# Two-layer decoder trunk on one core: the feed-forward's slab jobs handed out five at most at a time, partial sums parked through SyncE's queue, finished columns turned between slab jobs

## The chip, the core and the metric

The kernel runs on one core of one Trainium2 chip, in one launch. The metric is device time in microseconds (us), the median of three runs. A profile of one execution is read beside it. TensorE is called PE here (PEld is its weight load), VectorE DVE, ScalarE ACT, GpSimd POOL and SyncE SP, as in the profile.

## What is computed

The input has 256 tokens of width 2048. Each of two layers adds an attention-like mixer and then a feed-forward to the residual stream. The change concerns the feed-forward alone:

```
def squared_relu_mlp(h, w1, w2):
    z = jax.nn.relu(h @ w1)
    return (z * z) @ w2
...
        x = x + jnp.concatenate([token_out, mem_out], axis=-1) @ w_out[i]
        x = x + squared_relu_mlp(rms_norm(x, ffn_norm[i]), w_ff1[i], w_ff2[i])
```

`h` is 256x2048, `w1` 2048x8192 and `w2` 8192x2048, all float32. The kernel splits every float32 operand into a high part rounded to the fast matmul type and a low remainder, and adds the products high*high, low*high and high*low.

## The kernel before

All weights come from one DRAM array `in_w`, laid out in the order of use. The class `Feed` loads them through SP's queue into SBUF, ACT casts each block to its high part (line 170) and DVE subtracts to get the low part (line 173). The parts go into a ring of six 512-column places (`hi_ring`, `lo_ring`) and, in the feed-forward, two more (`slot`). Preparation runs at most three entries ahead of use.

The feed-forward (`ffn`) of a layer works on these pieces:

- **Up tiles** `("f", j)`, 64 of them. Each makes 128 of the 8192 hidden features with 32 matmuls into the PSUM bank `x_bank` (lines 919 and 921). ACT copies the bank out, and some 10 instructions on DVE and ACT, spread over the next ticks, turn two tiles into the squared values `z` (`convert`). A tick is four weight blocks of a tile, so an up tile has four.
- **Slab jobs** `("s", p, i, j)`. The product with `w2` is not done column by column: for most of it a Strassen-like scheme needs seven products in place of eight. One slab is the 2x2 block step for hidden chunk pair `i`: four jobs of 6, 3, 6 and 6 matmuls into seven PSUM banks `p` (lines 1010 to 1012). Its weights are a sum of blocks, so a slab needs two 512 KB loads through SP, `ra` and `rb`, and one 256 KB load that POOL's queue adds onto `ra` (line 141). Three SBUF buffers serve all slabs, so the `ra` of a slab can only be loaded when the slab two before it has been prepared to its last job.
- **Phases.** The seven banks hold one half of the output columns (A or B) for a run of slabs: `PHASES` lists half, first and last `i`. At the end of a phase `finish_banks` combines the seven banks on DVE and ACT into four corners (`c_x`, `c_y` and two parts of `room`; `c_a` and `c_b` in the last phase). If the half goes on later, the corners are parked in DRAM (`part`). If it has been parked before, the old sums are added back by accumulating loads on POOL's queue (called the gather here). When a half is complete, ACT scales the corners (line 1067), PE transposes them into the bank `ct`, and DVE adds them to the residual (line 1079); these steps are the turns.
- **Down tiles** `("d", 3, n)`, eight ordinary tiles at the end that use the hidden chunks that phase B leaves out.

`ffn_plan` writes the order: a credit of `RATE` = 4 jobs a tile is spent in the gap ahead of each up tile, a slab may start four tiles after its hidden pair was made, and the credit kept is at most 8. Steps that are written for a later time (`at(d, fn)`) run `d` ticks on. A scheduler below then orders each engine's instructions by its own estimates, so the place of an instruction in the queue of its engine is not simply that of the text.

An "end" below is the time around the end of a phase. Each layer has five: in this kernel after slab 7 (A), 14 (B), 21 (A), 24 (B, complete) and 32 (A, complete). Since all seven banks have to be emptied, a new phase starts one up tile later. Ahead of phase five the plan waits for four tiles (`hold = t + 4`), in which the B half is turned through the bank `t`.

While the feed-forward runs, half of the residual (`resid.parts[1]`, 1 MB) is stored to DRAM as `kept` (line 836), its SBUF place serves as two more spots for `z`, and it is loaded back at line 1112.

## Time and profile before

| | |
|---|---|
| median of three runs | 2095.45 us (2085.93 to 2096.34) |
| the profiled execution | 2087.09 us, its span 2085.2 us |
| PE busy | 2031.4 us, 97% |
| DVE, ACT, POOL busy | 85%, 66%, 9% |
| DMA | 439.80 MB, mean 211 GB/s |
| mean granted clock of TensorE | 0.991 |

The span is read in stretches: a row of the view by stretches gives its length, the busy time of each engine with the number of instructions in brackets, the mean granted clock (1.00 is full), the share of the DMA engines' time in use, and GB/s. The chain view follows the end of the program back from wait to wait; each row is a start in us, a length in us and what ran. A row such as "DMA slab<-in_w" is a transfer from its issue to its landing. Layer 0's feed-forward lies at about 236 to 963 us, layer 1's at about 1345 to 2085 us.

### The profile page before, as it was taken

How to read it: one execution, taken by the hardware profiler on the slowest of the kernel's cores; microseconds unless marked ns; L12 is line 12 of the kernel's file. 1: busy time of each engine (PE TensorE's matmuls, PEld its weight loads, DVE VectorE, ACT ScalarE, POOL GpSimd, SP SyncE). 2: the span in 40 equal slices, each digit the busy share in tenths (PEclk: the TensorE clock that was granted, in tenths of full speed). 3: DMA queues.
4: the chain of work that ended last, by engine and by line, in shares of the span. 5: the costliest groups of instructions: out<-in, count | busy, mean ns of one | idle time of the engine just before them, and what ended most of it. 6: DMA issues, size and time to landing. Idle time of an engine off the chain costs nothing.

```text
span 2085.2 us, 30357 instructions
## 1 busy us (share of the span) xinstructions
PE 2031.4 (97%) x10592; PEld 1713.7 (82%) x10592; DVE 1771.7 (85%) x2641; ACT 1373.1 (66%) x2177; POOL 178.8 (9%) x215
## 2 busy tenths in 40 slices
PE   9999999999999899999999999999999999999998
PEld 8888888788788687887888899888878878778787
DVE  8988788899889798998775798878889989888897
ACT  7765566576566566668665697566666666666664
POOL 0002300000000100000000000410000000101000
PEclk9999999999999999999999999999999999999999
DMA  8565666678677777676656645566677777868575
GB/s 310 176 205 186 217 213 209 208 228 233 209 224 230 212 225 209 213 206 202 213 184 195 194 144 177 192 223 212 209 220 234 223 217 225 233 211 241 177 224 171
DMA packets 133738, 439.80 MB, mean 211 GB/s; under 512 B 15248, under 2 KB 18320, under 8 KB 133072
## 3 DMA queue, kind: packets, MB, share of 16 engines
q1 hardware_dynamic: 112896, 395.90, 57.1%
q0 software_dynamic: 20544, 41.95, 11.0%
q8 instruction: 83, 1.36, 0.3%
q14 instruction: 71, 0.58, 0.1%
q10 hardware_dynamic: 144, 0.01, 0.0%
HBM read 424.56 MB, written 10.49 MB: 209 GB/s over the span
## 4 chain that ended last, share of the span: by engine, by line
PE 86%; DMA 5%; DVE 5%; ACT 2%; issue 2%; POOL 0%; DVEq 0%; ACTq 0%; POOLq 0%; SPq 0%
PE x_bank L919 19%; PE x_bank L921 9%; PE p L1012 7%; PE p L1010 7%; PE p L1011 7%; PE wo L503 6%; DMA slab<-in_w 3%; PE ff L919 3%; PE wo L505 3%; PE k L534 3%; PE v L534 3%; PE q L534 3%; PE u L503 2%; PE mk L534 2%; PE mv L534 2%
## 5 line engine op out<-in xcount | busy, mean ns | idle before, releaser
L173 DVE TENSOR_TENSOR lo_ring<-raw,hi_ring 128x512 fp32r<-128x512 f32 (+1 forms) x643 | 555.0, 879 | 108.2 <-ACT hi_ring L170 99.8
L170 ACT CAST hi_ring<-raw 128x512 fp32r<-128x512 f32 (+1 forms) x643 | 482.8, 766 | 202.8 <-PE wo L503 62.7
L170 ACT CAST hi_ring<-slab 128x1024 fp32r<-128x1024 f32 (+1 forms) x336 | 304.4, 906 | 135.6 <-DVE slab L204 60.9
L173 DVE TENSOR_TENSOR lo_ring<-slab,hi_ring 128x1024 fp32r<-128x1024 f32 (+1 forms) x336 | 346.9, 1043 | 44.2 <-ACT hi_ring L170 42.0
L141 POOL DMA_DIRECT2D slab<-in_w x112 | 97.2, 868 | 1655.5 <-DMA slab<-in_w 700.6
L170 ACT CAST slot<-slab 128x1024 fp32r<-128x1024 f32 x112 | 117.4, 1049 | 159.4 <-PE x_bank L919 109.4
L173 DVE TENSOR_TENSOR slot<-slab,slot 128x1024 fp32r<-128x1024 f32 x112 | 137.0, 1223 | 86.2 <-ACT slot L170 86.0
L919 PE MATMUL x_bank<-fx,hi_ring 128*128 128x512 f32 x664 | 209.4, 396 | 0.0
L503 PE MATMUL wo<-cat,hi_ring 128*128 128x512 f32 x512 | 161.6, 396 | 0.0
L921 PEld LDWEIGHTS x_bank<-fx,lo_ring 128*128 128x128 f32 x664 | 124.8, 188 | 29.5
L919 PE MATMUL x_bank<-fx0b,hi_ring 128*128 128x512 f32 x448 | 140.9, 395 | 0.0
L204 DVE TENSOR_TENSOR slab<-slab,slab 128x1024 f32<-128x1024 f32 x112 | 136.5, 1219 | 0.2
L933 ACT COPY room<-x_bank 128x512 f32<-128x512 f32 x112 | 65.4, 584 | 108.1 <-PE x_bank L921 108.1
L921 PE MATMUL x_bank<-fx,lo_ring 128*128 128x256 f32 x664 | 131.6, 278 | 0.0
L505 PEld LDWEIGHTS wo<-cat,lo_ring 128*128 128x128 f32 x512 | 96.1, 188 | 22.0
L919 PEld LDWEIGHTS x_bank<-fx,hi_ring 128*128 128x128 f32 x664 | 102.7, 189 | 4.9 <-ACT room L933 3.0
L173 DVE TENSOR_TENSOR slot<-raw,slot 128x1024 fp32r<-128x1024 f32 x70 | 85.5, 1222 | 19.7 <-ACT slot L170 19.5
L505 PE MATMUL wo<-cat,lo_ring 128*128 128x256 f32 x512 | 101.7, 278 | 0.0
L921 PEld LDWEIGHTS x_bank<-fx0b,lo_ring 128*128 128x128 f32 x448 | 84.2, 188 | 19.9
L1010 PE MATMUL p<-hi_ring,zb 128*128 128x512 f32 x230 | 91.0, 396 | 1.1 <-ACT hi_ring L170 0.9
L1011 PE MATMUL p<-hi_ring,zb 128*128 128x512 f32 x230 | 89.9, 391 | 0.0
L1012 PE MATMUL p<-lo_ring,zb 128*128 128x512 f32 x230 | 89.0, 390 | 0.0
(537 smaller groups left out, 4832.4 us busy)
## 6 DMA issues: line engine op xcount, KB each, us to landing
raw<-in_w SPq DMA_DIRECT2D x500, 512.0 KB, 4.4
slab<-in_w SPq DMA_DIRECT2D x224, 512.0 KB, 3.5
slab<-in_w POOLq DMA_DIRECT2D x112, 256.0 KB, 4.8
part<-room POOLq DMA_DIRECT2D x6, 512.0 KB, 3.8
resid_b<-kept SPq DMA_DIRECT2D x2, 1024.0 KB, 6.6
room<-part POOLq DMA_DIRECT2D x4, 512.0 KB, 8.4
memraw<-in_mem SPq DMA_DIRECT2D x4, 512.0 KB, 3.7
memraw<-in_mem SPq DMA_DIRECT2D x6, 256.0 KB, 6.0
```

Of the source, the lines that this page charges most:

```text
L141: self.nc.gpsimd.dma_start(t[:, 512:1024], self.wst[other, :, 512:1024], accum_op=ALU.add)
L170: cast = self.nc.scalar.copy(hi, src)
L173: self.nc.vector.tensor_sub(lo, src, hi.bitcast(F32))
L204: add(two, t.unsqueeze(1).to_broadcast([P, 2, 512]), two)
L503: nc.tensor.matmul(ps, hi, xs[:, k, :], start=first and j == 0, stop=False)
L505: nc.tensor.matmul(ps[:, T : 2 * T], lo, xs[:, k, 0:T], start=False, stop=last and j == len(ks) - 1,)
L534: nc.tensor.matmul(ps[t], a, b, start=i == 0 and j == 0, stop=i == NK - 1 and j == 2)
L919: nc.tensor.matmul(ps, hi, src(k), start=k == ks[0], stop=False)
L921: nc.tensor.matmul(ps[:, T : 2 * T], lo, src(k)[:, 0:T], start=False, stop=k == ks[-1])
L1010: nc.tensor.matmul(ps, al, hi[:, s], start=i == begin, stop=False)
L1011: nc.tensor.matmul(ps, ah, hi[:, s], start=False, stop=False)
L1012: nc.tensor.matmul(ps, ah, lo[:, s], start=False, stop=i == end - 1)
```

## The change

The numbers of the plan are new: the phases end after slab 6, 12, 18, 24 and 32, the rate is 4.5, and the credit kept is at most 5. So the gap after an end holds five jobs where it held eight. The wait of four tiles ahead of the last phase is gone. Its turns are now items of the plan, one in each of four gaps, after the gap's first slab job, and they go through the bank `st` that the up tiles use. Parking is issued on SP's queue (`nc.sync`) and is written five ticks after the end (nine where a gather comes first), and the gather five ticks after; scaling is written 9 ticks after the end of B and 11 after the end of A, where it was 8, and the last turns begin 13 ticks after, where it was 10. The last gather is two transfers and not three. The spill of the residual (`kept`, `more`) is removed.

How this stands in the queues, at two places. The first is the end of the third phase (A) in layer 0, on POOL before. `slab_6056` is the addition onto the `ra` of the new phase's second slab, `slab_6072` that of the third; `c_x<-part` is a gather, `part<-c_x` a park:

```order
L141 DMA slab_6056<-in_w 128x512
L1056 DMA c_x<-part_3726 128x512
L1056 DMA c_y<-part_3726 128x512
L1060 DMA part_6097<-c_x 128x512
L1056 DMA room_2624<-part_3726 128x1024
L1060 DMA part_6097<-c_y 128x512
L1060 DMA part_6097<-room_2624 128x1024
L141 DMA slab_6072<-in_w 128x512
```

On POOL now, where `slab_5591` is the second slab's `ra` and `slab_5654` the third's:

```order
L141 DMA slab_5591<-in_w 128x512
L1060 DMA c_x<-part_3592 128x512
L1060 DMA c_y<-part_3592 128x512
L1060 DMA room_2624<-part_3592 128x1024
L141 DMA slab_5654<-in_w 128x512
```

And on SP now, from the first slab's `rb` (`slab_5488`) to the third slab's `ra` (`slab_5654`); `slab_5597` is the second slab's `rb`:

```order
L139 DMA slab_5488<-in_w 128x1024
L139 DMA slab_5591<-in_w 128x1024
L139 DMA raw_5731<-in_w 128x1024
L1064 DMA part_5628<-c_x 128x512
L1064 DMA part_5628<-c_y 128x512
L139 DMA slab_5597<-in_w 128x1024
L1064 DMA part_5628<-room_2624 128x1024
L139 DMA raw_5798<-in_w 128x1024
L139 DMA slab_5654<-in_w 128x1024
```

The parks moved from POOL's queue to SP's, where two stand between the second slab's `ra` and `rb` and one ahead of the third slab's `ra`. The gather still stands right behind the second slab's addition on POOL. At the ends of phases one and two, which have no gather, all three parks stand on SP directly ahead of the second slab's `rb`.

The second place is the end of the fourth phase (B, complete) in layer 0, on ACT before; the scaling is line 1067, and the `raw` blocks are weights of up tiles:

```order
L170 CAST hi_ring<-raw_6868 128x1024
L933 COPY room_2624<-x_bank 128x512
L170 CAST hi_ring<-raw_6878 128x1024
L1067 ACTIVATE c_x<-c_x,d_x 128x512
L170 CAST slot_2625<-raw_6889 128x1024
L1067 ACTIVATE c_y<-c_y,d_x 128x512
L170 CAST hi_ring<-raw_6912 128x1024
L933 COPY room_2624<-x_bank 128x512
L902 CAST zb_2623<-room_2624 128x512
L1067 ACTIVATE room_2624<-room_2624,d_x 128x512 x2
```

On ACT now, where the scaling is line 1077, `slab_6499` and `slab_6509` are `ra` and `rb` of the last phase's first slab and `slab_6612` is the second slab's `ra`:

```order
L170 CAST hi_ring<-slab_6499 128x1024
L1044 COPY room_2624<-p_5684 128x512
L170 CAST slot_2625<-slab_6509 128x1024
L1077 ACTIVATE c_x<-c_x,d_x 128x512
L170 CAST hi_ring<-slab_6499 128x512
L933 COPY room_2624<-x_bank 128x512
L170 CAST hi_ring<-slab_6612 128x1024
L1077 ACTIVATE c_y<-c_y,d_x 128x512
L170 CAST hi_ring<-raw_6628 128x1024
L170 CAST hi_ring<-slab_6509 128x1024
```

The scaling had only preparation of up tiles around it; now the first scaling stands between the first slab's jobs, ahead of the cast for its second job (`slab_6499 128x512`), and the second ahead of the cast for its fourth (`slab_6509 128x1024`).

```diff
@@ -282,8 +282,8 @@
 
 STEPS = (1, 2, 3, 4, 6, 7, 8, 10)
 NB = 24
-PHASES = (("A", 0, 7), ("B", 0, 14), ("A", 7, 21), ("B", 14, 24), ("A", 21, 32))
-RATE = 4.0
+PHASES = (("A", 0, 6), ("B", 0, 12), ("A", 6, 18), ("B", 12, 24), ("A", 18, 32))
+RATE = 4.5
 
 
 def ffn_plan(tiles):
@@ -299,23 +299,30 @@
             ready[what[1] // 2] = t + LAG
     jobs = [(p, i, j) for p, (_, a, b) in enumerate(PHASES) for i in range(a, b) for j in range(4)]
     items = []
+    turns = {}
     credit = 0.0
     phase = hold = 0
     for t, what in enumerate(tiles):
-        credit = min(credit + RATE, 8.0)
+        credit = min(credit + RATE, 5.0)
         if what == ("d", 3, 0):
             credit = max(credit, 4.0)
+        first = len(items)
         while t >= hold and jobs and credit >= 1 and ready[jobs[0][1]] <= t:
             p, i, j = jobs[0]
             if p != phase:
                 items.append(("end", phase))
+                if PHASES[phase][2] == NB:
+                    turns = {t + 3 + h: h for h in range(4)}
                 phase = p
-                hold = t + (4 if PHASES[p - 1][2] == NB else 1)
+                hold = t + 1
                 break
             items.append(("s", *jobs.pop(0)))
             credit -= 1
             if not jobs:
                 items.append(("end", phase))
+        if t in turns:
+            assert len(items) - first > 2
+            items.insert(first + 1, ("turn", turns[t]))
         items.append(what)
     assert not jobs
     return items
@@ -832,18 +839,11 @@
         banks = []
         downs = [0]
         spots = [x[:, 2 * j : 2 * j + 2, :] for x in (za, zb) for j in range(8)]
-        kept = dp.tile([P, NK // 2, T], F32, tag="kept", name=f"kept{l}")
-        nc.sync.dma_start(kept, resid.parts[1])
-        more = sp.tile([P, 4, 512], F32R, tag="residb", name=f"more{l}")
-        spots += [more[:, 2 * j : 2 * j + 2, :] for j in range(2)]
         spare = list(range(len(spots)))
         zat, sat, due = {}, {}, {}
 
-        def take(late=False):
-            n = len(spots) - 2 if late else len(spots)
-            s = min(x for x in spare if x < n)
-            spare.remove(s)
-            return s
+        def take():
+            return spare.pop(0)
 
         def left(i, what):
             due[i].remove(what)
@@ -882,7 +882,7 @@
                 nc.scalar.activation(u, u, AF.Square)
 
             def high():
-                zat[i] = take(i >= 24)
+                zat[i] = take()
                 due[i] = ["A"] + (["B"] if i < NB else ["N"] * 8)
                 nc.scalar.copy(zs(i)[:, :, 0:T], u)
 
@@ -898,7 +898,7 @@
                 nc.vector.tensor_sub(s4, a12, s2)
 
             def sums_high():
-                sat[i] = take(i > 28)
+                sat[i] = take()
                 nc.scalar.copy(sit(i)[:, 0:512].rearrange("p (a c) -> p a c", a=2), sums)
 
             def sums_low():
@@ -1021,7 +1021,7 @@
             for p, tag in enumerate((*ms, "n0", "n1", "o", "t")):
                 banks.append(bk(tag, f"p{p}"))
 
-        part = {}
+        part, turns = {}, []
 
         def finish_banks(p):
 
@@ -1051,13 +1051,23 @@
             add(x3, x3, p4)
             whole = end == (32 if half == "A" else NB)
             sides = ((x0, 0), (x2, 1), (low, slice(2, 4)))
-            if begin:
+            if p == len(PHASES) - 1:
+                sides = ((upp, slice(0, 2)), (low, slice(2, 4)))
+            old = part.pop(half, None)
+
+            def gather():
                 for side, c in sides:
-                    nc.gpsimd.dma_start(side, part[half][:, c, :], accum_op=ALU.add)
+                    nc.gpsimd.dma_start(side, old[:, c, :], accum_op=ALU.add)
+
+            def park():
+                for side, c in sides:
+                    nc.sync.dma_start(part[half][:, c, :], side)
+
+            if old is not None:
+                at(5, gather)
             if not whole:
                 part[half] = dp.tile([P, 4, 512], F32, tag=f"part{half}{begin}", name=f"part{l}{p}")
-                for side, c in sides:
-                    nc.gpsimd.dma_start(part[half][:, c, :], side)
+                at(5 if old is None else 9, park)
                 return
 
             def scale():
@@ -1068,7 +1078,7 @@
 
             def turn(h):
                 c = 2 * h + 8 * (half == "A")
-                t4 = pp.tile([P, 2, T], F32, tag="t", bufs=1, name="ct")
+                t4 = bk("t" if half == "A" else "st", "ct", (P, 2, T))
                 for e in range(2):
                     n = (2 * h + e) // 4
                     w = (2 * h + e) % 4 * P
@@ -1081,9 +1091,13 @@
                     done(c)
                     done(c + 1)
 
-            at(8, scale)
+            if half == "B":
+                at(9, scale)
+                turns.append(turn)
+                return
+            at(11, scale)
             for h in range(4):
-                at(10 + h, lambda h=h: turn(h))
+                at(13 + h, lambda h=h: turn(h))
 
         tiles = [("f", j) for j in range(4 * NK)] + [("d", 3, n) for n in range(8)]
         items = ffn_plan(tiles)
@@ -1104,12 +1118,9 @@
                     runs[p, i](j)
                     if at_ < first_down and at_ >= ups:
                         tick()
-                    if (p, i, j) == (4, 29, 3):
-                        assert {16, 17} <= set(spare)
-                        resid.parts[1] = sp.tile(
-                            [P, NK // 2, T], F32, tag="residb", name=f"resid_b{l}"
-                        )
-                        nc.sync.dma_start(resid.parts[1], kept)
+                    continue
+                if what[0] == "turn":
+                    turns[0](what[1])
                     continue
                 if what[0] == "end":
                     finish_banks(what[1])
```

## The prediction

> **What bounds the kernel now.** I read the page first, then the busy time by stretches, then at each end of a phase the chain and the waits.
>
> ```profile
> PE 2031.4 (97%) x10592; PEld 1713.7 (82%) x10592; DVE 1771.7 (85%) x2641; ACT 1373.1 (66%) x2177; POOL 178.8 (9%) x215
> ```
>
> PE bounds the kernel, and the change takes no matmul away. What can be won is the time in which PE waits or is slowed. The stretches show where: first a quiet one, then the five ends of layer 0 (the fourth in two pieces), then those of layer 1.
>
> ```profile
> 600.00:690.00 90.00, 90.00 (x465) 76.41 (x464) 82.62 (x99) 63.06 (x82) 6.91 (x8) 1.00 0.78 233
> 385.00:425.00 40.00, 35.36 (x166) 27.59 (x165) 34.12 (x40) 24.05 (x30) 4.77 (x7) 1.00 0.67 205
> 540.00:590.00 50.00, 44.80 (x201) 34.03 (x200) 40.54 (x48) 30.18 (x39) 4.03 (x5) 0.97 0.65 198
> 695.00:750.00 55.00, 47.11 (x213) 36.58 (x213) 42.84 (x50) 31.11 (x39) 6.09 (x8) 0.94 0.72 212
> 806.00:837.00 31.00, 26.70 (x148) 23.11 (x148) 22.65 (x35) 17.26 (x25) 1.73 (x2) 0.94 0.61 175
> 837.00:870.00 33.00, 32.45 (x158) 26.45 (x157) 29.89 (x33) 21.78 (x27) 2.62 (x3) 1.00 0.69 218
> 940.00:963.00 23.00, 18.52 (x100) 15.73 (x99) 17.66 (x27) 13.91 (x23) 2.60 (x3) 0.93 0.78 218
> 1500.00:1540.00 40.00, 35.61 (x169) 27.76 (x168) 34.36 (x41) 23.73 (x29) 5.17 (x7) 1.00 0.67 208
> 1655.00:1705.00 50.00, 46.57 (x209) 36.45 (x208) 42.62 (x50) 31.45 (x39) 4.47 (x6) 0.93 0.72 214
> 1805.00:1860.00 55.00, 48.77 (x219) 37.61 (x217) 42.91 (x52) 29.68 (x37) 8.65 (x11) 0.94 0.74 208
> 1916.00:1952.00 36.00, 31.14 (x169) 26.81 (x168) 26.26 (x40) 19.82 (x29) 3.46 (x4) 0.91 0.61 181
> 2052.00:2078.00 26.00, 24.42 (x141) 20.80 (x140) 21.05 (x30) 13.05 (x17) 2.60 (x3) 1.00 0.63 168
> ...
> 641.61 0.63 PE L919 MATMUL x_bank<-fx0a,hi_ring 128*128 128x512 f32 x2
> ...
> 647.18 0.40 PE L1010 MATMUL p<-slot,za 128*128 128x512 f32 x1
> ```
>
> In the quiet stretch PE never idles, at 90/465 = 0.1935 us a matmul. The last two rows bracket one up tile of 32 matmuls: 5.57 us, or 0.174 each; a slab of 21 is then 53 x 0.1935 - 5.57 = 4.7 us. Length less matmuls at the quiet pace gives the loss at each end (0.174 in the fourth end's first piece, in layer 1's fourth end and in the fifth ends, where up or down tiles run alone). Layer 0: 7.9, 11.1, 13.8, 5.2 + 2.4 = 7.7, 5.6. Layer 1: 7.3, 9.6, 12.6, 6.6, 1.5. Together 83.7 us: no more can be won.
>
> What ends last there? The waits of PE at the first three ends of layer 0, and the chain at ends one and three:
>
> ```profile
> PE p L1010 <- ACT slot L170: 2.9, 2, 2.2
> ...
> PE p L1010 <- ACT slot L170: 3.8, 2, 3.0
> ...
> PE p L1010 <- ACT slot L170: 7.0, 2, 5.6
> ...
> 394.12 3.36 DMA slab<-in_w
> ...
> 398.12 7.40 DMA slab<-in_w
> 405.59 1.05 ACT slot L170
> ...
> 406.67 1.23 DVE L173 TENSOR_TENSOR slot<-slab,slot 128x1024 fp32r<-128x1024 f32 x1 [5.09 <-ACT slot L170]
> ...
> 700.98 7.30 DMA slab<-in_w
> ...
> 708.92 7.58 DMA slab<-in_w
> 716.57 1.05 ACT slot L170
> ...
> slab<-in_w SPq DMA_DIRECT2D x224, 512.0 KB, 3.5
> ...
> slab<-in_w POOLq DMA_DIRECT2D x112, 256.0 KB, 4.8
> ```
>
> Each time it is the third slab of the new phase: its `ra` is loaded once the first slab is fully prepared, then the addition, then the cast. At end one that takes 3.36 + 7.40, at end three 7.30 + 7.58, against medians of 3.5 and 4.8. PE waits 2.9, 3.8 and 7.0 us for it. The rest of the loss is PE running at the pace of preparation.
>
> **The change part by part.** *Five jobs a gap.* The third slab's first job is asked for after the same PE work as before: then up tile, 8 jobs, up tile; now up tile, 5 jobs, up tile, 3 jobs. So its wait stays: 2.9, 3.8 and 7.0. What changes is that three jobs of the second slab and three of the third get an up tile (5.57 us) of cover. Of the 11 jobs that ran at preparation pace, 5 keep it, so I keep 5/11 of the rest. Layer 0: 2.9 + 5/11 x 5.0 = 5.2, 3.8 + 5/11 x 7.3 = 7.1, 7.0 + 5/11 x 6.8 = 10.1; layer 1 with the same waits 4.9, 6.4, 9.5. Saved: 32.8 - 22.4 = 10.4 and 29.5 - 20.8 = 8.7, in all 19.1 us. The bounds: nothing, if DVE's work only comes due elsewhere, and the whole 62.3 of these six ends.
>
> *Parking through SP.* POOL's rows at end three, with the start of the up tile that follows the phase:
>
> ```profile
> 688.80 0.62 PE L919 MATMUL x_bank<-fx0a,slot 128*128 128x512 f32 x2
> ...
> 691.94 1.22 POOL L1056 DMA_DIRECT2D c_x<-part  x1
> ...
> 698.26 0.58 POOL L1060 DMA_DIRECT2D part<-c_x  x1 [3.47 <-DMA c_x<-part]
> 698.83 0.90 POOL L1056 DMA_DIRECT2D room<-part  x1
> ...
> 707.11 0.55 POOL L1060 DMA_DIRECT2D part<-room  x1 [6.81 <-DMA room<-part]
> ```
>
> At ends one and two the parks now stand on SP ahead of the second slab's `rb`, which waits for a buffer anyway, and their data are combined by then: cost nothing, gain nothing, since "later" in the text moves them little in the queue. If that cover went, `rb` would come late by the issue of three transfers. At end three SP waits in order for the gather: the first park until about 698.3, the last until `room` has landed. The `room` gather no longer stands behind a park, so it is issued some 3 us sooner and lands near 704, not 707.1. Then the third slab's `ra`, at 700.98 before, can only follow at about 704.6. It starts 3.6 us later and, with the gather gone, should land 2 to 4 us quicker, and the addition likewise: between 4 us won and 4 us lost, and I take nothing.
>
> A rule speaks against the queue as such. The rows 7.30 and 7.58 hold 6.6 us of crowding; were it POOL's queue alone, both layers would win 13 us more and the time would be some 2053. The Trainium skill ("DMA: Bandwidth & Descriptors", Issuing engines are not separate DMA queues) says that transfers from all queues run on the same 16 DMA engines and interleave, so that another queue saves only issue time. By that rule the crowding stays. The trace cannot decide it, and my sum does not contain the 13.
>
> *The fourth end.* The wait of four tiles goes, so the last phase starts like the others, with a third slab to wait for. New is that ACT's scaling stands among the first slab's casts and waits there for the gather. The price, from the scaling before:
>
> ```profile
> 812.68 0.72 ACT L1067 ACTIVATE c_x<-c_x,d_x 128x512 f32<-128x512 f32 x1 [5.46 <-DMA c_x<-part]
> ...
> 815.76 0.72 ACT L1067 ACTIVATE c_y<-c_y,d_x 128x512 f32<-128x512 f32 x1 [1.42 <-DMA c_y<-part]
> ```
>
> At end three `c_x` landed 698.26 - 688.80 = 9.5 us after the phase. The second job is asked for after an up tile and the first job's 6 matmuls of 21, at 5.57 + 4.7 x 6/21 = 6.9; its cast is ready after the scaling and about as long again, at 9.5 + 0.7 + 0.7 = 10.9: 4.0 us lost. `c_y` adds about 1.4, the third slab's first wait stays near 2.9, and four turns through the up tiles' bank may cost 1 (each has four transposes and a DVE addition, under three or four jobs):
>
> ```profile
> L1076 PE MATMUL ct<-const,room x16: 272/273/421, 819.7 to 1946.9; 128*128 128x128 f32 x16
> ...
> L1079 DVE TENSOR_TENSOR resida<-resida,ct x8: 678/680/689, 825.2 to 1947.2; 128x512 f32<-128x512 f32 x8
> ```
>
> That makes 9.3 a layer, where 7.7 and 6.6 were lost: 4.3 us dearer in both. Its bounds are nothing lost at all and the third rival below. Transposes, additions and scalings keep their number.
>
> *The fifth end.*
>
> ```profile
> PE ct L1076 <- ACT c_b L1067: 6.0, 2, 4.5
> ...
> 949.82 8.78 DMA c_b<-part
> ```
>
> PE's first turn waits 4.5 and 1.5 us for the last gather. POOL has nothing else left, so the gather starts as before, when the corners are combined; the turn comes three ticks later, 3/4 x 5.57 = 4.2 us. Saved: 4.2 and 1.5. One more down tile follows, so nothing is added at the end of the program.
>
> *The spill.* Four transfers of 1 MB go; they lay under matmuls, with no wait of PE behind them: nothing.
>
> The sum: 19.1 - 4.3 + 5.7 = 20.5 us. 2087.09 (the profiled execution, span 2085.2) - 20.5 = 2067. The runs shown lie in pairs, at 2086 to 2087 and 2095 to 2096, and the median is in the upper; the changed kernel's may fall in either, so I name 2070.
>
> **The rivals.** *The ends all but vanish* (three us each, 30 in all): 2087 - 54 = 2033. For it: DVE idled 5.09 us at end one, so preparation has room. Against: the third slab's deadline is unchanged. *The waits only move*: preparation for the up tile now comes ahead of the deferred jobs, and DVE (34 of 40 us busy at end one) is late for that instead. Then the time is within 0.5% of the median (10 us, about what a measurement here can tell): 2085 to 2106. For it: DVE's rows at end one, 27 from the first to the last of these, show no idle time between them:
>
> ```profile
> 379.25 0.29 DVE L898 TENSOR_TENSOR room<-room 128x128 f32<-128x128 f32 x1
> ...
> 400.36 1.22 DVE L173 TENSOR_TENSOR lo_ring<-slab,hi_ring 128x1024 fp32r<-128x1024 f32 x1
> ```
>
>  *Slower*: ACT's scaling at the fourth end. If its waits (5.46 + 1.42 = 6.9) hold up the first slab, and through the release of `ra` the third and the fifth again, and each turn costs 1.2 on the up tile, the end costs 9.3 + 2 x 6.9 + 4 x 1.2 = 27.9 a layer: 2087 - 24.8 + 20.2 + 21.3 = 2104 or, in the upper pair, 2113. It cancels the other 24.8 us from about 19.6 us a layer on.
>
> **How the numbers follow.** The partial gain (2040 to 2085) gets 0.62, the vanishing ends (below 2040) 0.12, the moved waits 0.15, slower 0.11. So faster 0.74, same 0.15, slower 0.11. The range, 2040 to 2097, leaves out the vanishing ends, the dear fourth end and little more; the likeliest case alone spans 2048 to 2085.
>
> **What would show it.** Right: at the first three ends of each layer PE still waits for a cast behind a slab's addition, but loses about 5, 7 and 10 us; at the fourth, ACT's scaling of `c_x` idles for its gather in front of a cast for a slab; at the fifth PE's wait for `c_b` is under 1 us. Wrong: additions of third slabs that land in 4.8 us at ends one to three, a fourth end above 20, or new waits in the gaps between ends, where 4.5 jobs leave DVE less room.

## The result and the profile after

The changed kernel takes 2149.72 us (median of 4 runs, 2147.32 to 2159.05), the kernel before beside it 2092.36 (2085.93 to 2096.34): a ratio of 1.0285, with a 95% interval of 1.0243 to 1.0328. It is slower by 57 us. The prediction said 2070, faster; its range ended at 2097. The profiled execution after took 2149.27 us (span 2147.4), the one before 2087.09 (span 2085.2), so the two traces differ by 62 us.

The busy row of the page after:

```profile
PE 2054.5 (96%) x10592; PEld 1715.0 (80%) x10592; DVE 1770.8 (82%) x2641; ACT 1374.6 (64%) x2177; POOL 166.6 (8%) x195
```

The work is the same: as many matmuls, and PEld, DVE and ACT as busy as before to 2 us. The rest is waiting (PE's own busy time grew by 23 us for the same matmuls, so it holds some of that), and the stretches show where. First come the ends and the gaps between them in layer 0 after, then those of layer 1; each end stands as far behind its phase's first corner copy, and is as long, as the one shown before (the fourth of layer 0 is one piece now, the fifths are longer because the turn comes later).

```profile
369.00:409.00 40.00, 37.15 (x179) 30.14 (x178) 34.39 (x40) 23.76 (x30) 3.43 (x4) 0.96 0.72 215
409.00:513.00 104.00, 98.23 (x478) 80.21 (x477) 87.36 (x105) 64.57 (x82) 7.79 (x9) 0.97 0.68 208
513.00:563.00 50.00, 44.73 (x210) 35.66 (x209) 40.77 (x47) 29.41 (x37) 3.46 (x4) 0.97 0.71 209
563.00:653.00 90.00, 86.19 (x431) 70.21 (x431) 78.12 (x94) 58.05 (x76) 8.18 (x10) 1.00 0.68 208
653.00:708.00 55.00, 47.79 (x223) 37.54 (x222) 42.20 (x48) 29.75 (x38) 4.87 (x6) 0.97 0.78 222
708.00:789.00 81.00, 78.01 (x389) 63.69 (x388) 71.28 (x84) 55.41 (x71) 6.06 (x7) 1.00 0.72 218
789.00:853.00 64.00, 56.30 (x275) 45.66 (x274) 51.58 (x63) 37.50 (x49) 7.39 (x9) 0.95 0.71 194
853.00:940.00 87.00, 83.54 (x420) 67.97 (x419) 74.87 (x87) 56.07 (x71) 6.54 (x8) 1.00 0.72 217
957.00:1000.00 43.00, 35.88 (x195) 31.03 (x194) 32.97 (x55) 26.55 (x45) 1.73 (x2) 0.92 0.54 162
1515.00:1555.00 40.00, 37.01 (x178) 29.85 (x177) 34.93 (x41) 23.78 (x30) 3.43 (x4) 0.96 0.72 210
1555.00:1659.00 104.00, 98.19 (x483) 79.82 (x482) 87.27 (x106) 64.43 (x82) 7.79 (x9) 0.98 0.70 212
1659.00:1709.00 50.00, 44.64 (x204) 35.74 (x203) 39.96 (x45) 28.52 (x36) 3.46 (x4) 0.93 0.68 205
1709.00:1793.00 84.00, 81.93 (x412) 67.29 (x411) 74.15 (x90) 57.03 (x73) 6.05 (x7) 1.00 0.71 217
1793.00:1848.00 55.00, 46.58 (x207) 36.02 (x206) 41.23 (x48) 28.84 (x36) 6.08 (x7) 0.91 0.71 202
1848.00:1931.00 83.00, 81.03 (x409) 66.67 (x408) 71.85 (x85) 54.19 (x69) 6.92 (x8) 1.00 0.72 221
1931.00:1967.00 36.00, 32.23 (x151) 26.65 (x150) 29.80 (x38) 21.93 (x29) 5.22 (x6) 0.91 0.75 197
1967.00:2090.00 123.00, 115.77 (x586) 94.41 (x586) 104.19 (x123) 77.65 (x99) 8.68 (x10) 1.00 0.71 210
2102.00:2140.00 38.00, 34.95 (x203) 30.39 (x202) 27.80 (x40) 16.93 (x22) 1.73 (x2) 1.00 0.51 151
```

At nine jobs in two gaps, and with the tile and slab times of the prediction, a quiet matmul takes (2 x 5.57 + 9/4 x 4.7) / 111.25 = 0.195 us. Length less matmuls at that pace is the loss. Ends one to three lose 5.1, 9.0 and 11.5, then 5.3, 10.2 and 14.6: 55.7 us, where 62.3 were lost before. The gaps between the ends lose 10.8, 6.0, 5.1 and 5.1 in layer 0 and 9.8, 3.7, 3.2 and 8.7 in layer 1: 52.4 us. Before, at 0.1935, the eight gaps lost 3.2 us in all, 2.0 of them in the last. Three of the rows of before:

```profile
425.00:540.00 115.00, 115.00 (x596) 97.82 (x596) 106.02 (x127) 78.14 (x102) 10.65 (x13) 1.00 0.79 232
870.00:936.00 66.00, 65.92 (x339) 55.51 (x338) 62.56 (x79) 44.72 (x59) 5.21 (x6) 1.00 0.75 221
1952.00:2050.00 98.00, 97.92 (x496) 82.18 (x495) 90.89 (x106) 64.42 (x79) 7.80 (x9) 1.00 0.74 227
```

The granted clock is not the main reason: six of the eight gaps of after have 1.00 and lose 31.8 us. The fourth ends lose 10.4 and 6.6 (7.7 and 6.6 before, in pieces at 0.1935 and 0.174), the fifth 9.1 and 2.7 at 0.174 (5.6 and 1.5). Less 6.6, plus 52.4 - 3.2 = 49.2, plus 2.7 and 4.7, that is 50 of the 62 us; this count does not place the other 12. Nearly all of the 50 lie where the prediction's sum has no term.

What ACT waits for says the same. Its waits for the loads of a slab, the addition among them, before and then after:

```profile
ACT slot L170 <- DMA slab<-in_w: 35.8, 8, 9.3
ACT hi_ring L170 <- DMA slab<-in_w: 1.5, 2, 1.1
```
```profile
ACT hi_ring L170 <- DMA slab<-in_w: 74.2, 24, 8.0
ACT slot L170 <- DMA slab<-in_w: 17.5, 10, 3.0
```

The columns are us in total, times and longest. Ten waits of 37 us in all, at the first three ends, became 34 of 92 us. One of the new ones, with the two slabs' loop that it belongs to, from the rows of SP, POOL, ACT and DVE; first two slabs in the quiet stretch of before, then in a gap of after:

```profile
588.74 0.33 SPq L139 DMA_DIRECT2D slab<-in_w  x1
592.67 0.86 POOL L141 DMA_DIRECT2D slab<-in_w  x1 [9.72 <-DMA slab<-in_w]
599.55 1.05 ACT L170 CAST slot<-slab 128x1024 fp32r<-128x1024 f32 x1
607.52 1.23 DVE L173 TENSOR_TENSOR lo_ring<-slab,hi_ring 128x1024 fp32r<-128x1024 f32 x1 [0.17 <-ACT hi_ring L170]
```
```profile
573.76 6.00 SPq L139 DMA_DIRECT2D slab<-in_w  x2
580.17 0.86 POOL L141 DMA_DIRECT2D slab<-in_w  x1 [10.89 <-DMA slab<-in_w]
587.83 1.05 ACT L170 CAST hi_ring<-slab 128x1024 fp32r<-128x1024 f32 x1 [5.93 <-DMA slab<-in_w]
599.32 1.22 DVE L173 TENSOR_TENSOR slot<-slab,slot 128x1024 fp32r<-128x1024 f32 x1
599.43 0.33 SPq L139 DMA_DIRECT2D slab<-in_w  x1
```

A slab has two buffers, and there are three. So the first buffer of the next slab but one is loaded when a slab's last subtraction gives its second buffer back: load, addition, first cast, last subtraction, and round again. Before, that loop took from 588.74 to 608.75, 20.0 us for two slabs. This is not the shortest that it could take: while PE is never kept waiting, a round takes on average what PE asks for, which is two slabs each 2 x 53 x 0.1935 = 20.5 us. The room is inside the round. It is the time that a first buffer lies finished before ACT takes it up. The addition issued at 592.67 landed 5.0 us later, at 597.6, and the cast began at 599.55, 1.9 us after that. Over 42 slabs of layer 0 the median is 1.9 too.

After, PE asks for two slabs each 2 x (5.57 / 1.125 + 4.7) = 19.3 us, which would leave 0.7 of the 1.9 us if nothing in the round grew. The loop shown takes 25.7 (the median in layer 0 is 22.5); the cast begins 0.15 us after the landing, and ACT has idled 5.93 us for it. In 18 of those 42 slabs the cast now begins within 0.2 us of the landing, where before it was 5.

### The profile page after: what moved, and what is told of

Same layout as the page of the kernel before. It is cut to its first block, busy times and chain, and to the rows that moved or that the text cites. A ratio compares the mean times of both kernels' runs of the same rounds, so it can differ in the third digit from the quotient of the medians.

```text
span 2147.4 us, 30368 instructions
## 1 busy us (share of the span) xinstructions
PE 2054.5 (96%) x10592; PEld 1715.0 (80%) x10592; DVE 1770.8 (82%) x2641; ACT 1374.6 (64%) x2177; POOL 166.6 (8%) x195
## 3 DMA queue, kind: packets, MB, share of 16 engines
q1 hardware_dynamic: 114912, 398.00, 55.7%
## 5 line engine op out<-in xcount | busy, mean ns | idle before, releaser
L919 PE MATMUL x_bank<-fx,hi_ring 128*128 128x512 f32 x704 | 224.7, 398 | 0.0
L921 PEld LDWEIGHTS x_bank<-fx,lo_ring 128*128 128x128 f32 x704 | 132.2, 189 | 38.3 <-DVE lo_ring L173 7.7
L921 PE MATMUL x_bank<-fx,lo_ring 128*128 128x256 f32 x704 | 140.1, 280 | 4.6 <-DVE lo_ring L173 4.6
L1010 PE MATMUL p<-hi_ring,zb 128*128 128x512 f32 x280 | 114.2, 408 | 15.2 <-ACT hi_ring L170 14.7
L919 PE MATMUL x_bank<-fx0b,hi_ring 128*128 128x512 f32 x408 | 128.1, 395 | 0.0
L1012 PE MATMUL p<-lo_ring,zb 128*128 128x512 f32 x280 | 111.1, 407 | 8.4 <-DVE lo_ring L173 8.1
L919 PEld LDWEIGHTS x_bank<-fx,hi_ring 128*128 128x128 f32 x704 | 111.0, 190 | 6.7 <-ACT room L933 3.4
L1011 PE MATMUL p<-hi_ring,zb 128*128 128x512 f32 x280 | 110.8, 396 | 0.0
L933 ACT COPY room<-x_bank 128x512 f32<-128x512 f32 x118 | 68.8, 583 | 52.4 <-PE x_bank L921 51.9
L919 PE MATMUL x_bank<-fx0a,hi_ring 128*128 128x512 f32 x296 | 97.3, 404 | 0.0
```

The source lines that it names most:

```text
L919: nc.tensor.matmul(ps, hi, src(k), start=k == ks[0], stop=False)
L921: nc.tensor.matmul(ps[:, T : 2 * T], lo, src(k)[:, 0:T], start=False, stop=k == ks[-1])
L933: nc.scalar.copy(pairs[j // 2 % 3][:, 512 * (j % 2) : 512 * (j % 2) + 512], ps)
L1010: nc.tensor.matmul(ps, al, hi[:, s], start=i == begin, stop=False)
L1011: nc.tensor.matmul(ps, ah, hi[:, s], start=False, stop=False)
L1012: nc.tensor.matmul(ps, ah, lo[:, s], start=False, stop=i == end - 1)
```

## The experiments

Labels that begin with `a_` change the changed kernel, `b_` the kernel before, `i_` the changed kernel at RATE 4.0 with the cap at 8.0, `c_` two things at once; `x_` takes a suspected cost away from the changed kernel. Every ratio is to the kernel before on the same chip.

**Which part carries the loss.** `a_rate4`, `a_rate4c5`, `a_cap8`; and `b_rate45`, which gives the kernel before the same two numbers:

```diff
-RATE = 4.5                                  (a_rate4 and a_rate4c5)
+RATE = 4.0
-        credit = min(credit + RATE, 5.0)    (a_rate4 and a_cap8)
+        credit = min(credit + RATE, 8.0)
```

> The changed kernel with RATE 4.0 and the cap of the credit at 8.0, as before the change; the shorter phases, the parking through SyncE, the turns between slab jobs and the later last turn stay. Theory 'slab chain': a slab's two buffers of three come back only after load, addition, cast and preparation, some 20.5 us for two slabs, so slabs can follow each other about every 10.2 us; PE asks for one every 10.2 us at four jobs a gap and every 9.65 us at 4.5, and waits for the difference. Then this kernel's stretches between the ends are quiet again and it takes 2080 to 2105 us. Theory 'ends': the parking, the turns among the slabs and the later last gather cost the time; then it stays above 2125 us. Theory 'split': what costs is that a slab's four jobs lie in two gaps; there are whole slabs again here, so the time falls as by the first.

> The changed kernel with RATE 4.0 alone; the cap stays at 5.0, so the phase begins with a gap of five and every slab after it lies in two gaps (one job, then three). Theory 'slab chain': the rate counts and not the split; 2080 to 2110 us. Theory 'split': slabs that lie in two gaps come late at any rate; above 2130 us. Theory 'ends': above 2125 us.

> The changed kernel with the cap of the credit at 8.0 alone: a phase begins with a gap of eight jobs, as before the change, then 4 and 5 by turns. Theory 'slab chain': the chain is as far behind as with the cap of 5, since the number of slabs in a stretch is the same; 2140 to 2165 us. If the five-job cap does at the ends what the prediction gave it (19 us), it is 15 to 20 us slower than the changed kernel; if the cap does nothing, within 5 us of it.

> The kernel before with RATE 4.5 and the cap 5.0 alone; its phases, its parking on GpSimd's queue, its wait of four tiles at the fourth end and its turns stay. Theory 'slab chain': the slowdown comes with the rate, 2125 to 2155 us. Theory 'ends': 2070 to 2095 us, since the rate spares what the prediction gave it.

Measured: `a_rate4` 2091.68 us, ratio 0.9992 (0.9978 to 1.0006); `a_rate4c5` 2134.46, 1.0208 (1.0185 to 1.0230); `a_cap8` 2155.62, 1.0303 (1.0279 to 1.0326); `b_rate45` 2171.44, 1.0388 (1.0368 to 1.0409). So the rate and the cap carry the whole loss, and at the old rate and cap all the rest of the change together is worth nothing. At the new ones it is not: `b_rate45`, slower than expected, is 22 us above the changed kernel, and no run takes these apart. `a_cap8` is 6 us above the changed kernel, with overlapping intervals: no more than this is what the cap, and with it the first gap of five, is worth at a rate of 4.5. The prediction had 19. Three gaps of `a_rate4` are quiet again at the old pace of 0.1935:

```profile
400.00:500.00 100.00, 99.83 (x515) 84.47 (x514) 92.13 (x110) 68.62 (x88) 8.58 (x10) 1.00 0.78 232
530.00:630.00 100.00, 100.00 (x517) 85.01 (x516) 91.88 (x110) 69.13 (x89) 7.77 (x9) 1.00 0.78 233
690.00:765.00 75.00, 75.00 (x388) 63.68 (x388) 68.52 (x81) 52.19 (x68) 6.05 (x7) 1.00 0.78 234
```

My first form of the theory, that only the rate counts, fell with `a_rate4c5`: with four jobs a gap as before, but most slabs split over two gaps (one job, then three), it loses 43 us. By the plan 40 of a layer's 56 slabs are split there, 24 in the changed kernel and none in `a_rate4` and before. So the split alone is enough for a loss; how the 58 us of the changed kernel divide between split and rate is not shown. The split makes the loop longer. Over 42 slabs of layer 0, from rows like those above: SP's start to the landing of the addition takes 10.0 us on average in `a_rate4` and 10.7 in `a_rate4c5`; first cast to last subtraction 10.1 and 11.4; and between landing and first cast lie 1.8 us in the median in the one, 0.2 in the other. The round grew by 0.7 + 1.3 = 2.0 us, and the room was 1.8.

**Is it the loop of the buffers?** `x_noadd` leaves the addition out, `x_rows4` adds a fourth slab buffer and takes one of the four raw buffers away for it.

```diff
-                self.nc.gpsimd.dma_start(                           (x_noadd)
-                    t[:, 512:1024], self.wst[other, :, 512:1024], accum_op=ALU.add
-                )
-SLOTS, AHEAD, LOADS, KOFF, RAWS = 6, 3, 3, 2, 4                     (x_rows4)
+SLOTS, AHEAD, LOADS, KOFF, RAWS = 6, 3, 3, 2, 3
-                t = self.rows.tile([P, 1024], F32, tag="rows", bufs=3, name=f"slab{h}")
+                t = self.rows.tile([P, 1024], F32, tag="rows", bufs=4, name=f"slab{h}")
...                                          (the other tiles of this tag likewise)
```

> The changed kernel (4.5 jobs, cap 5) without the DMA that adds the second half of another row to a slab's first buffer, so that a part of the feed-forward's sums is left out; what goes is GpSimd's addition, 4 to 8 us of each slab's chain, and 29 MB of 436 MB. Theory 'slab chain' (now with the split in it: a slab that lies in two gaps gives its buffers back an up tile's preparation later, so that two slabs take some 22 us where the whole ones took 20.5): the chain falls by about 5 us a slab, below what PE asks for, and the stretches between the ends are quiet again; 2045 to 2095 us. Theory 'order' (the split costs because ACT's and DVE's pieces for the up tile and the slab stand in a bad order, whatever the buffers do): above 2125 us.

> The changed kernel with four slab buffers in place of three, and three raw buffers in place of four to make room for them. Theory 'slab chain': a slab's first buffer no longer waits for the slab before the last to be prepared in full, so it is loaded and added up to 10 us earlier; most of the 58 us come back, 2080 to 2115 us, unless the missing raw buffer costs something of its own. Theory 'order': the buffers don't matter, above 2135 us.

Measured: `x_noadd` 2049.99 us, 0.9803 (0.9786 to 0.9820); `x_rows4` 2092.17, 1.0004 (0.9990 to 1.0017). Both keep 4.5 jobs, the cap of 5 and the split slabs, and neither has the loss. In `x_rows4` one kind of ACT's waits for slabs is left, at the ends:

```profile
ACT slot L170 <- DMA slab<-in_w: 23.1, 7, 8.2
```

Over the same 42 slabs load and addition take 10.4 us there on average and first cast to last subtraction 11.0, as long as in the changed kernel (10.3 and 10.9). But between landing and cast lie 2.2 us in the median, where the changed kernel has 0.8. That settles the cause: the longer pieces stayed and the loss did not, so it was the wait for the buffer and not the order of ACT's and DVE's pieces. `x_noadd` moves 29 MB less as well, so its 2050 us is no price of the loop alone.

**A shorter loop by other means.** The first buffer in two transfers, the half that is added to first: `i_halves`, `a_halves`, `b_halves`.

```diff
-            step = 512 if self.lp == 0 else 1024
-            for c in range(0, n, step):
+            first = r[0] == "S" and r[2] == 0
+            step = 512 if self.lp == 0 or first else 1024
+            for c in sorted(range(0, n, step), reverse=first):
```

> The changed kernel with RATE 4.0 and cap 8.0 (2091.7 us), and a slab's first buffer loaded in two transfers, the half that is added to first, so that the addition can start when 256 KB have landed and not 512. Theory 'slab chain': the third slab of a phase is ready 1 to 2 us sooner at eight ends, 2076 to 2089 us. If the transfers share the same engines and only change places, no change: 2089 to 2096 us.

> The changed kernel, 4.5 jobs and cap 5, with the slab's first buffer loaded in two halves and nothing else. Theory 'slab chain': the addition starts 1 to 2 us sooner for each of 56 slabs a layer, and where PE waits in all stretches the whole of that counts, so a good part of the 58 us comes back: 2105 to 2130 us. Theory 'order': 2140 to 2150 us.

> The kernel before with the slab's first buffer loaded in two halves and nothing else. Theory 'slab chain': only the ends gain, as in the run of the two halves on the changed kernel's phases (2080.0 us there): 2076 to 2086 us. If the shorter phases and the other parts of the change carried that gain, 2090 to 2096 us.

Measured: `i_halves` 2080.03 us, 0.9944 (0.9922 to 0.9966); `a_halves` 2132.77, 1.0185 (1.0168 to 1.0203); `b_halves` 2085.32, 0.9969 (0.9956 to 0.9981). The loss follows the loop by degrees, but `a_halves` misses its range: 17 us came back, not 20 to 45. The sizes of the queues' transfers in `i_halves` (KB each, median us to landing) bear on why the gain is small:

```profile
slab<-in_w SPq DMA_DIRECT2D x224, 256.0 KB, 3.3
slab<-in_w SPq DMA_DIRECT2D x112, 512.0 KB, 3.4
```

A load of 256 KB, with its other half issued right beside it, lands hardly sooner than one of 512 KB. The Trainium skill ("DMA: Bandwidth & Descriptors", Anatomy of one DMA — SWDGE (gpsimd) path) gives a DMA on GpSimd's path about 2.0 us fixed plus its bytes at 436 GB/s, so that by an estimate from it 256 KB less would save 0.6 us; on SP's queue, which that figure is not for, the rows here save 0.1. Of the kernels that do the whole work `i_halves` is the fastest: 0.6% under the one before, 3.2% under the changed one.

The same order of loads can be shifted further: `i_early` and `a_early` are `i_halves` and `a_halves` with the next slab's first buffer loaded ahead of this slab's second.

```diff
-                self.loads += [("S", p[1], 0), ("S", p[1], 1)]
+                n = p[1]
+                self.loads += [("S", i, 0) for i in (n, n + 1) if i // 56 == n // 56]
+                self.loads = list(dict.fromkeys(self.loads)) + [("S", n, 1)]
```

> The changed kernel, 4.5 jobs and cap 5, with the two halves, and the next slab's first buffer loaded ahead of this slab's second one, so that it takes the buffer that comes free at the addition to the second buffer and not the one that comes free after the last preparation, some 4 us later. Theory 'slab chain': two slabs' loop falls by about 4 us, and most of the 58 us come back: 2060 to 2095 us. If the second buffer, now loaded last, becomes the limit (its load, 3.3 to 4.5 us, then stands in every slab's own way), it stays above 2115 us.

> The same order of loads with RATE 4.0 and cap 8.0 and the two halves (2080.0 us without the new order). Theory 'slab chain': only the ends can gain: 2062 to 2080 us. By the prediction's first term this is slower than the kernel with 4.5 jobs and the same loads by 10 to 20 us; if the second buffer becomes the limit, 2085 us or more.

Measured: `a_early` 2236.82 us, 1.0706 (1.0685 to 1.0726); `i_early` 2166.23, 1.0356 (1.0333 to 1.0379). This is the second outcome of each text, and far above its bound. Rows of SP and ACT in `i_early`, where SP's row with x2 is a first buffer in halves, the one with x1 behind it a second buffer, and the x3 both for the next slab:

```profile
443.33 0.81 SPq L142 DMA_DIRECT2D slab<-in_w  x2
...
445.68 0.33 SPq L142 DMA_DIRECT2D slab<-in_w  x1
```
```profile
451.31 1.05 ACT L173 CAST slot<-slab 128x1024 fp32r<-128x1024 f32 x1 [0.18 <-DMA slab<-in_w]
```
```profile
455.92 3.20 SPq L142 DMA_DIRECT2D slab<-in_w  x3
```

The second buffer is now loaded at 445.68, after the last subtraction of the slab ahead; the cast from it runs at 451.31 as it lands, and the next second buffer starts at 455.92 + 3.20 - 0.33 = 458.8. That is 13.1 us for a slab, where PE asks for one each 10.25. The next one takes 10.0 us; long and short rounds alternate, so that two slabs take 23.1 us where PE asks for 20.5.

**The other parts of the change.** `i_pool` undoes the parking of unfinished halves, `i_end5` the later last end, both at RATE 4.0 and cap 8.0; `b_end4` does the fourth end's part alone in the kernel before.

```diff
-                    nc.sync.dma_start(part[half][:, c, :], side)    (i_pool)
+                    nc.gpsimd.dma_start(part[half][:, c, :], side)
-                at(5, gather)
+                at(5, gather) if whole else gather()
-                at(5 if old is None else 9, park)
+                park()
-            at(11, scale)                                           (i_end5)
+            at(8, scale)
-                at(13 + h, lambda h=h: turn(h))
+                at(10 + h, lambda h=h: turn(h))
-                at(5, gather)
+                at(5, gather) if p < 4 else gather()
-                hold = t + (4 if PHASES[p - 1][2] == NB else 1)     (b_end4)
+                hold = t + 1
...
+            items.insert(first + 1, ("turn", turns[t]))
...
+                if p == 3:
+                    at(5, gather)
...
+            if half == "B":
+                at(9, scale)
+                turns.append(turn)
+                return
```

> The changed kernel with RATE 4.0 and cap 8.0 (2091.7 us), and the parking of the three unfinished halves a layer undone: gathered and parked through GpSimd's queue at once, as before the change. The prediction took nothing for this part, with 4 us either way at third ends; if it holds, 2088 to 2096 us. If parks on GpSimd's queue held back the slab additions behind them, undoing the part loses up to 13 us: 2097 to 2105 us.

> The changed kernel with RATE 4.0 and cap 8.0, and the last end of a layer as before the change (gather at once, scaling at tick 8, turns from tick 10). The trace of the kernel without this edit loses 9.0 and 5.7 us more or less at the fifth ends of the two layers, the kernel before lost 6.8 and 2.6; if the three ticks are the reason, it gains about 6 us: 2083 to 2088 us. If the turns wait for the gather anyway, no change: 2089 to 2096 us.

> The kernel before with the fourth end's part of the change alone: no wait of four tiles, gather at tick 5, scaling at tick 9, turns between slab jobs into the up tiles' bank. The prediction called it 4.3 us a layer dearer: 2098 to 2104 us. By the rival of the prediction (ACT's scaling holds up the first slabs) 20 us a layer: 2120 to 2140 us. If the wait of four tiles was worth as much as the scaling costs, no change: 2088 to 2096 us.

Measured: `i_pool` 2091.53 us, 0.9990 (0.9980 to 1.0000); `i_end5` 2091.46, 0.9997 (0.9982 to 1.0011); `b_end4` 2094.73, 1.0010 (0.9995 to 1.0025), beside 2091.68 for `a_rate4` and 2093.4 for the kernel before. None of the three parts can be told from nothing. The text ahead of `b_end4` gives the prediction's price as 4.3 us a layer; the prediction has 9.3 a layer against 7.7 and 6.6, so 4.3 us for both layers together.

**The prediction's first term by itself.** `c_r45` and `c_r40` have the halves, four slab buffers and three raw buffers; the one keeps 4.5 jobs and cap 5, the other has 4.0 and 8.0. `i_57` and `i_48` are `i_halves` with at most five and four jobs in a phase's first gap:

```diff
+        most = 5 if phase and t == hold else 8                      (i_57; 4 in i_48)
-        while t >= hold and jobs and credit >= 1 and ready[jobs[0][1]] <= t:
+        while len(items) - first < most and t >= hold and jobs and credit >= 1 and ready[jobs[0][1]] <= t:
```

> The changed kernel (4.5 jobs a gap, cap 5) with the slab chain shortened in both ways: the first buffer loaded in two halves, and four slab buffers and three raw buffers. The chain no longer binds, so this and the next run weigh the prediction's first term by itself: five jobs at a phase's first gap against eight. By the prediction's term it is 10 to 20 us faster than the next run; if the term is empty, within 5 us of it. In all 2065 to 2090 us; the three raw buffers cost some 15 us outside the feed-forward by the trace of the run with four slab buffers.

> The changed kernel with RATE 4.0 and cap 8.0, the first buffer in two halves, four slab buffers and three raw buffers. With the chain out of the way what is left at a phase's start is eight jobs prepared at the preparation's own pace: 2075 to 2095 us. By the prediction's first term it is 10 to 20 us slower than the same kernel with 4.5 jobs and cap 5; if the term is empty, within 5 us.

> The changed kernel with RATE 4.0, cap 8.0 and the two halves (2080.0 us), and at most five jobs in the first gap of a phase, so that the gaps are 5, 7, 4, 4 and only the second slab lies in two of them. By the prediction's first term, three jobs of the second slab get an up tile of cover at eight ends, 1.5 us each: 2062 to 2075 us. If the chain gives that back at the third slab, no change: 2076 to 2084 us.

> The same with at most four jobs in the first gap, so that the gaps are 4, 8, 4, 4 and no slab lies in two. If the cover of the second slab is what counts, all four of its jobs get it: 2060 to 2075 us. If the waits only move to the third and fourth slab, which are now asked for in one gap, no change or worse: 2076 to 2090 us.

Measured: `c_r45` 2098.24 us, 1.0024 (1.0011 to 1.0037); `c_r40` 2115.54, 1.0102 (1.0087 to 1.0117); `i_57` 2094.12, 0.9993 (0.9982 to 1.0005); `i_48` 2096.69, 1.0019 (1.0008 to 1.0031). All four are above their expected ranges. ACT's waits for slabs in `c_r40`, `c_r45`, `i_halves` and `i_57`, one fence each:

```profile
ACT slot L171 <- DMA slab<-in_w: 44.2, 8, 10.2
ACT hi_ring L171 <- DMA slab<-in_w: 1.8, 2, 1.6
```
```profile
ACT slot L171 <- DMA slab<-in_w: 21.5, 6, 7.4
ACT hi_ring L171 <- DMA slab<-in_w: 1.5, 1, 1.5
```
```profile
ACT slot L171 <- DMA slab<-in_w: 28.7, 7, 7.0
ACT hi_ring L171 <- DMA slab<-in_w: 8.6, 8, 2.5
```
```profile
ACT hi_ring L171 <- DMA slab<-in_w: 30.1, 20, 6.1
ACT slot L171 <- DMA slab<-in_w: 22.8, 16, 4.2
```

With four buffers the lower cap and the higher rate win 17 us, and the waits fall by 23. With three buffers and the same halves the same two numbers lose 53 us: `a_halves` takes 2132.77 and `i_halves` 2080.03. So the same edit has opposite signs on the two sides of the loop. (The kernels with four slab buffers also have a raw buffer less.) A shorter first gap by itself doesn't help with three buffers either: five or four jobs cost 14 and 17 us over the eight of `i_halves`, and in `i_57` the waits rise from 37 us in 15 to 53 in 36. `i_48` splits no slab, so what it loses is not the split; what it is stays open.

How much of the 17 us is the cap and how much the rate wasn't taken apart. Nor was the price of the raw buffer that the `c_` kernels gave up: `c_r40` is 24 us slower than `a_rate4`, for whose phases and rates it has a buffer more and the halves besides. And `c_r45`, which differs from `x_rows4` by the halves alone, is 6 us slower than it; why isn't known.

## Why the prediction was wrong

**What bounds the kernel: right, but read too shortly.** PE bounds it, and the stretches found the losses at the ends. The step that failed is the sentence that in the quiet stretch PE never idles, taken as though preparation had room there. The sum has no term for the stretches between the ends at 4.5 jobs; the last line names waits there as something that would make it wrong, without a price. They cost 52.4 us, where they had cost 3.2. The rows of before held part of it: a first buffer lies finished for 1.9 us in each round of two slabs, and the higher demand alone, 19.3 us for two slabs where it was 20.5, takes 1.2 of them. What the prediction did not ask is what a split does to the loop. In `a_rate4c5` the split made it 2.0 us longer and cost 43 us at the old rate; in the changed kernel split and rate come together. Why the split lengthens load and preparation by 0.7 and 1.3 us a slab stays open.

**Five jobs a gap: mis-sized.** Predicted 19.1 us saved at ends one to three; the trace after shows 62.3 - 55.7 = 6.6, and `a_cap8` 6 by the whole time. End one came out as forecast: 5.1 and 5.3 us lost, for 5.2 and 4.9. Ends two and three lost 9.0 to 14.6 us each, where 6.4 to 10.1 were forecast, since the third slab, and at end three the second with it, waits on the same loop. Only with a fourth buffer did cap and rate win 17 us. The prediction's line that the third slab's wait stays, being asked for after the same work of PE, left out that the slabs behind it are on the same loop.

**Parking through SP: right.** Taken as nothing, measured as nothing: the parks on either queue give 2091.5 and 2091.7 us. The two effects that the prediction set against each other are there, too. At the third ends of `a_rate4` SP waits for the gather, so the third slab's load starts 5.1 and 4.4 us after the last subtraction ahead of it, against 1.8 in `i_pool`. Load and addition together then take 10.5 us in both layers, against 15.4. So the addition lands some 2 us sooner, which the time doesn't show. The prediction set the Trainium skill ("DMA: Bandwidth & Descriptors", Issuing engines are not separate DMA queues) against the 13 us of crowding. The equal times don't decide for that rule: the crowding mostly went, and the later start used up most of what it gave. Since the edit moved the transfers in time as well as to another queue, no run here shows what the queue alone does.

**The fourth end: right, with the size within the noise.** ACT's scaling waits for its gather among the first slab's casts, as predicted, and PE behind it; rows of ACT over the run and of PE from 784 to 858 us after:

```profile
ACT c_x L1077 <- DMA c_x<-part: 12.2, 2, 6.4
```
```profile
PE p L1010 <- ACT hi_ring L170: 6.4, 4, 4.4
```

Predicted 4.3 us dearer for both layers together. The part alone measures 1.3 us in all, with an interval from 1 us won to 5 us lost, which holds both nothing and the 4.3; the trace after has 2.7. The slower rival, 20 us a layer and more, is out.

**The fifth end: wrong.** Predicted 5.7 us saved. PE's wait for `c_b` did shrink, from 4.5 to 0.6 us, but the next one took its place. The waits of PE from 950 to 1000 us after, then from 936 to 975 in `i_end5`:

```profile
PE ct L1086 <- DVE residb L1089: 6.5, 1, 6.5
PE ct L1086 <- ACT c_b L1077: 0.6, 1, 0.6
```
```profile
PE ct L1086 <- ACT c_b L1077: 3.4, 1, 3.4
PE ct L1086 <- DVE residb L1089: 0.8, 1, 0.8
```

Three ticks later the second turn needs the bank that DVE has not read yet, and DVE has other work in front. The prediction did not ask what was late next. Either way the time is the same, 2091.68 us in `a_rate4` and 2091.46 in `i_end5`.

**The spill: not contradicted.** No run takes it out alone; with everything else but rate and cap it lies in the 0.9992 of `a_rate4`.

**The rivals.** The ends did not vanish and ACT's scaling did not decide. "The waits only move, DVE late instead" came nearest, but it is not DVE that is late: ACT's added 55 us of waits are for slab loads, and with a fourth buffer the same work on DVE is in time. What is late is the buffer. No rival had a place for that.

## What to carry to other kernels

A stretch without a wait is no proof of slack. Follow one buffer round its loop (load, addition, cast, last use, next load). The length of the loop says little, since it follows the consumer as long as nobody waits; what counts is how long the finished buffer lies before it is taken up. Here that was 1.9 us in some 20. A change that raises the demand, or that spreads a job's use of the buffer over more time, by more than this room is paid for round after round, and what shortens the loop pays as often. And an edit that smooths bursts is worth its price only where the buffer behind it has room: here the same two numbers cost 53 us with three buffers and won 17 with four.

## What the runs showed of the hardware

Splitting a load in two brought a half in hardly sooner than a whole one (3.3 us for 256 KB, 3.4 for 512 KB, medians on SP's queue in `i_halves`; 3.5 and 3.4 in `a_halves`), where the two halves are issued one behind the other. Under another order of loads the difference was larger (3.0 and 4.3 us in `i_early`). The adding DMA on POOL's queue took 4.8 to 6.8 us for 256 KB (medians over the runs), longer than a plain load of the same size on SP's queue in any run (3.0 to 3.5 us).
